# A third buffer for the doubled queries in the second attention block of a diffusion-backbone layer on one Trainium2 core

## The chip, the cores and the metric

One core of one Trainium2 chip runs the whole kernel in one launch. The metric is device time in microseconds (us), the median of several runs. Engines are named as in the profile: PE (TensorE), DVE (VectorE), ACT (ScalarE), POOL (GpSimd), and SP, which here only issues DMAs.

## What is computed

One layer over 256 context tokens and 2048 latent tokens (a grid of 32 rows by 64 columns), model width 1024, float32. An input projection feeds three mixers: 2-D neighbourhood attention, a gated recurrence in both directions and a short convolution. They are merged by sigmoid gates and projected out. The change concerns the neighbourhood attention of the latent tokens alone:

```python
# 8 heads of 64; windows of 8 rows x 16 columns; queries in blocks of 16 columns
s_loc = einsum('brnqhd,brnikhd->brnhqik', q_blk, k_band)       # 8 x 32 keys around the block
s_ctx = einsum('brnqhd,bchd->brnhqc', q_blk, ctx_k)            # 256 cached context keys
s = concatenate([s_loc * scale + bias, s_ctx * scale], -1)     # learned bias per head, mask
p = softmax(s, -1)
o = p_loc @ v_band + p_ctx @ ctx_v
```

## The kernel before

**Precision.** Every dense product splits its operands into a high and a low part and sums three passes. For attention scores, queries are stored in DRAM as `d_q[512, 2, T]`, each row holding the high and the low part. The function `twice` (L654) reads one head's rows twice, so that all 128 partitions hold them: these are the doubled queries `qs`, a tile of 128 x 2 x 512 floats, 512 KB. The keys `kd` hold high parts in partitions 0 to 63 and low parts in 64 to 127.

**Two blocks.** [...] The first block's attention has query group 0 alone (pool `atA`); the second block's (pool `atB`) has groups 1, 2 and 3. A group is 8 grid rows, 512 queries. A job is one group of one head, in the order of `jobs` (head 0 groups 1, 2, 3, then head 1 and so on: 24 jobs), written here as (group, head). A job has four units, one for each block of 16 columns (b = 0 to 3).

**A unit** (`attend1` and on): PE computes the scores `sc` against the context keys (L583) and `sl` against the local keys (L587), both from `qs`; DVE moves them out of PSUM with a row maximum (L588, and L590, which adds the bias `bt`); ACT takes the exponential (L596); DVE scales by the reciprocal sum (L598). Two units later PE transposes the probabilities `p` (L611), ACT copies them out (L614), and after that PE multiplies them with the values (L624) into `o`. `fin` (L757) multiplies a job's `o` with its gate `sg` on DVE (L762) and stores `zt`.

**Loads.** All loads of this stage are issued from POOL's queue. After unit b = 0 of a job, the loads of the next job are written: `load_group` (L725) loads `qs`, for a new head's group 1 and group 3 the bias `bt`, and the gate `sg`; at a change of head `load_head` (L711) comes first with `kd` and the cached keys `ck`, and `load_values` (L720) follows after b = 3. Tiles of `atB` have two buffers by default; `sg` has three. A load waits for the last reader of the buffer that it overwrites, and whatever stands behind it in POOL's queue waits too. POOL also computes the low parts of the dense weights (`wlo`, L56).

**Order of the work.** The attention units are put between the dense column tiles 40 + m, m = 4 to 17 (`ps`, L153, 24 matmuls for each of two token chunks) by `Side`, 101 steps over 27 chunks. The framework's scheduler then fixes one order for each engine's queue, from its own costs and from which buffers it expects to be free; at run time each engine works its queue in that order.

Of the kernel before, what the change touches and what calls it, by code (L numbers as in the profile page):

```python
# [9 lines left out]
F32R = mybir.dt.float32r  # L10
# [5 lines left out]
P = 128  # L16
# [28 lines left out]
def build(nc, tc, H):  # L45
# [5 lines left out]
    def r2f(ap):  # L51
        return ap.bitcast(F32)
# [598 lines left out]
    def rows(h):  # L651
        return slice(h * HD, h * HD + HD)

    def twice(h, t0, n):  # L654
        return d_q[rows(h), :, t0 : t0 + n].unsqueeze(0).broadcast_to([2, HD, 2, n])
# [46 lines left out]
    def latent_steps(at, gs):  # L702

        cv = at.tile([P, 2, 512], F32, tag="cv", name=f"cv{gs[0]}", bufs=1)
        row0 = GR[gs[0]][1]
        nrows = GR[gs[-1]][1] + GR[gs[-1]][2] - row0
        nrow_max = max(GR[g][2] for g in gs)
        nq = (nrows + 3) // 4
        heads, groups, bias = {}, {}, {}

        def load_head(h):  # L711

            kd = at.tile([P, nrows * 64], F32R, tag="kd", name=f"kd{row0}_{h}")
            t0 = 256 + row0 * 64
            G.dma_start(r2f(kd), d_k[h, :, :, t0 : t0 + nrows * 64].rearrange("a p n -> (a p) n"))
            ck = at.tile([P, 256], F32R, tag="ck", name=f"ck{row0}_{h}")
            G.dma_start(r2f(ck), d_ck[h].rearrange("a p n -> (a p) n"))
            heads[h] = [kd, ck, None]

        def load_values(h):  # L720
            vb = at.tile([P, nq, 4, HD], F32, tag="vb", name=f"vb{row0}_{h}")
            G.dma_start(vb, d_vb[h][:, row0 // 4 : row0 // 4 + nq])
            heads[h][2] = vb

        def load_group(g, h):  # L725
            _, _, nrow, bi = GR[g]
            qs = at.tile([P, 2, 512], F32R, tag="qs", name=f"qs{g}_{h}")
            G.dma_start(r2f(qs), twice(h, 256 + 512 * g, 512))
            if (bi, h) not in bias:
                bt = at.tile([P, 3, nrow_max * 32], F32, tag="bt", name=f"bt{bi}_{h}")  # L730
                G.dma_start(bt[:, :, : nrow * 32], H[f"bias{bi}"][h])
                bias[bi, h] = bt
            sg = at.tile([HD, 512], F32, tag="sg", name=f"sg{g}_{h}", bufs=3)
            G.dma_start(sg, d_gna[rows(h), 256 + 512 * g : 768 + 512 * g])
            groups[g, h] = qs, bias[bi, h], sg

        jobs = [(g, h) for h in range(HEADS) for g in gs]

        def first_loads():
            load_head(0)  # L740
            load_group(*jobs[0])
            G.dma_start(cv, H["cv"].rearrange("(a p) c -> p a c", p=P))
            load_values(0)

        return first_loads, latent_units(at, jobs, heads, groups, cv, row0, load_head, load_group, load_values)

    def latent_units(at, jobs, heads, groups, cv, row0, load_head, load_group, load_values):
# [163 lines left out]
    with tc.tile_pool(name="zp", bufs=2, reuse_waits="tile") as zp:  # L911
        for c in (0, 1, 2, 3, 4):
# [5 lines left out]
            for br in (2, 1, 0):  # L918
# [6 lines left out]
                for m in range(8):  # L925
                    t = zp.tile([P, 512], F32, tag="acc" if br == 2 else "tg", name=f"tg{c}_{br}_{m}",
                                bufs=9 if br == 2 else 6)
# [148 lines left out]
```

## Time and profile before

| | us |
|---|---|
| median of 3 runs (lowest to highest) | 2610.14 (2605.08 to 2614.53) |
| the profiled execution's own time | 2611.47 |
| its span, first to last instruction | 2609.7 |
| mean granted TensorE clock, share of full | 0.985 |
| second block's attention, where it runs beside the dense tiles | about 1576 to 2025 of the span |
| loads of `qs` in the profile | 32 (8 in the first block, 24 in the second) |

Times in rows are us from the start of the span. The span is some 2 us shorter than the execution's own time. [...] Where a row says that an engine was idle until something, that is the event that came last by the profile.

### The profile page before, as it was taken

To read this page: it belongs to the slowest core of one execution; us is meant where nothing else is said; L and a number is where in the kernel's file an instruction comes from. 1 tells how busy PE (TensorE), PEld (TensorE's weight loads), DVE (VectorE), ACT (ScalarE), POOL (GpSimd) and SP (SyncE) were. 2 spreads that over 40 slices of the span, in tenths; PEclk is the share of its full clock that TensorE was granted. 3 is DMA by queue.
4 is the path that set the end of the run, shared out by engine and by line. 5 is a ranking of instruction groups with operands and counts; after the bars stand their busy time and mean duration, and the time that the engine had idled before them with its cause. 6 is when DMAs were issued, how large, how long until landed. Compare 5 with 4: busy or idle time off the path is not lost.

```text
span 2609.7 us, 35312 instructions
## 1 busy us (share of the span) xinstructions
PE 2542.3 (97%) x13192; PEld 2077.4 (80%) x13192; DVE 1104.2 (42%) x2329; ACT 978.3 (37%) x1849; POOL 876.7 (34%) x757
## 2 busy tenths in 40 slices
PE   8999999999999999999999997999999999999998
PEld 4887788888878888888888886777777888888887
DVE  5101245555123331325777863455444134333433
ACT  4312443444223334436665653444444311111221
POOL 2311223323532321522544443233231413334642
PEclk9999999999999999999999998999899999999999
DMA  7335642332733434435642335455442466545442
GB/s 275 112 87 159 170 122 81 68 70 69 188 106 119 148 121 145 133 101 135 190 156 91 115 121 179 136 146 151 131 137 77 155 224 200 177 157 186 159 141 88
DMA packets 248812, 360.84 MB, mean 138 GB/s; under 512 B 88761, under 2 KB 124729, under 8 KB 247617
## 3 DMA queue, kind: packets, MB, share of 16 engines
q1 hardware_dynamic: 147360, 227.20, 28.7%
q0 software_dynamic: 47920, 64.26, 8.8%
q10 hardware_dynamic: 53360, 67.13, 7.8%
q8 instruction: 104, 1.70, 0.3%
q14 instruction: 68, 0.55, 0.1%
HBM read 248.10 MB, written 110.11 MB: 137 GB/s over the span
## 4 chain that ended last, share of the span: by engine, by line
PE 75%; DMA 6%; issue 4%; POOL 2%; DVE 1%; ACT 0%; SPq 0%; ACTq 0%; POOLq 0%; DVEq 0%
PE ps L153 45%; PE pb L932 12%; PE po L981 8%; DMA qs<-d_q 3%; PE t L611 3%; PE o L624 2%; PE pg L454 2%; PE pv L321 1%; PE sl L587 1%; PE sc L583 1%; DMA bt<-bias 1%; DMA d_z<-sp 1%; POOL wlo L56 0%; DMA kp<-d_k 0%; DMA d_q<-evl 0%
## 5 line engine op out<-in xcount | busy, mean ns | idle before, releaser
L153 PE MATMUL ps<-xh,whi 128*128 128x512 f32 (+1 forms) x2400 | 899.6, 375 | 0.0
L153 PE MATMUL ps<-xl,whi 128*128 128x512 f32 (+1 forms) x2400 | 888.8, 370 | 2.4 <-DVE xl L56 1.6
L153 PE MATMUL ps<-xh,wlo 128*128 128x512 f32 (+1 forms) x2400 | 888.2, 370 | 0.0
L153 PEld LDWEIGHTS ps<-xh,whi 128*128 128x128 f32 x2400 | 455.2, 190 | 93.7 <-issue 6.2
L56 POOL TENSOR_TENSOR wlo<-wraw,whi 128x512 fp32r<-128x512 f32 x240 | 334.0, 1409 | 570.0 <-ACT whi L55 505.3
L153 PEld LDWEIGHTS ps<-xh,wlo 128*128 128x128 f32 x2400 | 455.1, 190 | 78.1
L153 PEld LDWEIGHTS ps<-xl,whi 128*128 128x128 f32 x2400 | 455.2, 190 | 77.8 <-POOL xl L56 2.0
L55 ACT CAST whi<-wraw 128x512 fp32r<-128x512 f32 x240 | 144.8, 616 | 300.1 <-PE ps L153 160.9
L932 PE MATMUL pb<-zh,wbh 128*128 128x512 f32 (+1 forms) x480 | 179.0, 373 | 4.3 <-ACT zh L55 4.3
L167 ACT ACTIVATE evm<-ps 128x512 f32<-128x512 f32 (+1 forms) x120 | 66.3, 552 | 301.1 <-PE ps L153 300.2
L932 PE MATMUL pb<-zl,wbh 128*128 128x512 f32 (+1 forms) x480 | 179.1, 373 | 0.0
L932 PE MATMUL pb<-zh,wbl 128*128 128x512 f32 (+1 forms) x480 | 179.0, 373 | 0.0
L588 DVE TENSOR_SCALAR_CACHE_REDUCE p<-sc 128x256 f32<-128x256 f32 x127 | 53.9, 424 | 254.1 <-PE sc L583 253.1
L939 POOL TENSOR_TENSOR tg<-tg,tg 128x512 f32<-128x512 f32 (+1 forms) x80 | 96.9, 1221 | 188.5 <-DVE tg L935 184.3
L935 DVE SCALAR_TENSOR_TENSOR tg<-tg,pb 128x512 f32<-128x512 f32 (+1 forms) x120 | 74.7, 631 | 151.8 <-PE pb L932 139.8
L611 PE MATMUL t<-ident,p 128*128 128x128 f32 (+1 forms) x698 | 129.4, 286 | 7.0 <-DVE ast L595 3.4
L611 PEld LDWEIGHTS t<-ident,p 128*128 128x128 f32 (+1 forms) x698 | 91.6, 142 | 53.9 <-issue 19.6
L614 ACT COPY pT<-t 128x512 f32<-128x512 f32 (+3 forms) x256 | 96.2, 406 | 75.0 <-PE t L611 74.7
L596 ACT ACTIVATE p<-p,ast 128x736 f32<-128x736 f32 (+2 forms) x127 | 109.4, 862 | 39.5 <-DVE ast L595 38.1
L444 DVE SCALAR_TENSOR_TENSOR uf<-ut,pk,uf 128x512 f32<-128x512 f32 (+1 forms) x120 | 103.0, 858 | 30.5 <-ACT uf L441 28.6
L475 POOL TENSOR_TENSOR sq<-sq,ea 128x512 f32<-128x512 f32 (+1 forms) x40 | 61.9, 1548 | 154.2 <-ACT sq L468 92.6
L55 ACT CAST zh<-zr 128x512 fp32r<-128x512 f32 (+1 forms) x60 | 30.5, 575 | 211.8 <-PE pb L932 92.6
(233 smaller groups left out, 3689.7 us busy)
## 6 DMA issues: line engine op xcount, KB each, us to landing
wraw<-w_in SPq DMA_DIRECT2D x240, 256.0 KB, 3.4
d_sig<-evm ACTq DMA_DIRECT2D x96, 256.0 KB, 3.5
tg<-d_sig SPq DMA_DIRECT2D x96, 256.0 KB, 3.8
xt<-x SPq DMA_DIRECT2D x36, 512.0 KB, 3.7
qs<-d_q POOLq DMA_DIRECT2D x32, 512.0 KB, 17.1
zr<-d_z SPq DMA_DIRECT2D x12, 1024.0 KB, 5.4
d_mrg<-tg ACTq DMA_DIRECT2D x32, 256.0 KB, 4.4
mr<-d_mrg SPq DMA_DIRECT2D x8, 1024.0 KB, 5.8
```

The lines of the kernel that those rows point to most:

```text
L55: S.copy(hi, src)
L56: lo_eng.tensor_tensor(lo, src, r2f(hi), ALU.subtract)
L153: TE.matmul(ps[:, :n], (lo if a else hi)[:, k, :], (xl if b else xh)[ci][:, k, :], start=(i == 0), stop=(i == len(ps_) - 1))
L167: S.activation(o[:, :n], ps, AF.Tanh, scale=0.5)
L444: V.scalar_tensor_tensor(uf[:, :n], ut[:, tap : tap + n], cw(tap), uf[:, :n], ALU.mult, ALU.add)
L596: S.activation(p[:, :nk], p[:, :nk], AF.Exp, bias=st[:, 2:3], accum_out=st[:, 3:4])
L611: TE.transpose(tb[:, off : off + w], p[q0:q1, c0 : c0 + P], ident[q0:q1, q0:q1])
L614: S.copy(pT[:, base : base + off], tb[:, :off])
L932: TE.matmul(ps[:, :n], (wbl if a_ else wbh)[br * 4 + k][:, m * P : (m + 1) * P], (zl if b_ else zh)[:, k, :n], start=(i == 0), stop=(i == ...
L935: V.scalar_tensor_tensor(t[:, :n], t[:, :n], 1.0, ps[:, :n], ALU.add, ALU.mult)
L939: G.tensor_tensor(acc[m][:, :n], acc[m][:, :n], t[:, :n], ALU.add)
L981: TE.matmul(ps, (ml if a_ else mh)[:, k, j * P : (j + 1) * P], (wol if b_ else woh)[k][:, hs], start=(i == 0), stop=(i == len(ps_) - 1))
```

## The change

`qs` gets three buffers instead of two where the stage has more than one group, that is, in the second block; the first block keeps two.

```diff
         def load_group(g, h):
             _, _, nrow, bi = GR[g]
-            qs = at.tile([P, 2, 512], F32R, tag="qs", name=f"qs{g}_{h}")
+            qs = at.tile([P, 2, 512], F32R, tag="qs", name=f"qs{g}_{h}",
+                         bufs=3 if len(gs) > 1 else 2)
             G.dma_start(r2f(qs), twice(h, 256 + 512 * g, 512))
```

One line is added, so lines behind L728 have numbers higher by one. The queues of PE, DVE, ACT and SP hold the same instructions in the same order as before. On POOL's queue the loads of `qs` move. The number of instructions is the same on every engine.

POOL's queue around the change from head 0 to head 1, before (`qs2_1` is the load of `qs` for group 2 of head 1):

```order
L56 TENSOR_TENSOR wlo47_14386<-wraw47_0_14387,whi47_14385 128x512
L728 DMA qs3_0_13682<-d_q_57 128x2x512
L56 TENSOR_TENSOR wlo47_14386<-wraw47_1_14391,whi47_14385 128x512
L734 DMA sg1_1_13863<-d_gna_62 64x512
L728 DMA qs1_1_13859<-d_q_57 128x2x512
L731 DMA bt1_1_13861<-bias1 128x1440
L734 DMA sg2_1_14021<-d_gna_62 64x512
L717 DMA ck4_2_14352<-d_ck_59 128x256
L728 DMA qs2_1_14019<-d_q_57 128x2x512
L731 DMA bt2_1_14189<-bias2 128x3x384
L715 DMA kd4_2_14350<-d_k_58 128x1792
```

And in the changed kernel:

```order
L729 DMA qs1_1_13859<-d_q_57 128x2x512
L56 TENSOR_TENSOR wlo47_14386<-wraw47_0_14387,whi47_14385 128x512
L56 TENSOR_TENSOR wlo47_14386<-wraw47_1_14391,whi47_14385 128x512
L735 DMA sg1_1_13863<-d_gna_62 64x512
L729 DMA qs2_1_14019<-d_q_57 128x2x512
L732 DMA bt1_1_13861<-bias1 128x1440
L735 DMA sg2_1_14021<-d_gna_62 64x512
L717 DMA ck4_2_14352<-d_ck_59 128x256
L729 DMA qs3_1_14187<-d_q_57 128x2x512
L732 DMA bt2_1_14189<-bias2 128x3x384
L715 DMA kd4_2_14350<-d_k_58 128x1792
```

To within a row or two, each place that held a load of `qs` still holds one, but that of the next job: where `qs1_1` stood in front of `bt1_1`, `qs2_1` stands now; where `qs2_1` stood behind `ck4_2`, `qs3_1` stands now. So each load of `qs` is moved ahead of the rows that stood between two of them. The same pattern holds for the later heads.

The first loads of the stage, POOL's queue before:

```order
L722 DMA vb4_0_13362<-d_vb_61 128x1792
L728 DMA qs2_0_13548<-d_q_57 128x2x512
L734 DMA sg2_0_13550<-d_gna_62 64x512
L731 DMA bt2_0_13684<-bias2 128x3x384
L734 DMA sg3_0_13686<-d_gna_62 64x512
L715 DMA kd4_1_13855<-d_k_58 128x1792
```

And in the changed kernel:

```order
L722 DMA vb4_0_13362<-d_vb_61 128x1792
L729 DMA qs2_0_13548<-d_q_57 128x2x512
L735 DMA sg2_0_13550<-d_gna_62 64x512
L729 DMA qs3_0_13682<-d_q_57 128x2x512
L732 DMA bt2_0_13684<-bias2 128x3x384
L735 DMA sg3_0_13686<-d_gna_62 64x512
```

Here the third load of `qs` goes out with the first batch, ahead of the second bias table.

## Rows read from the trace of the kernel before

**Rows 1.** The page: busy time of the engines; the chain that ended last.
```profile
PE 2542.3 (97%) x13192; PEld 2077.4 (80%) x13192; DVE 1104.2 (42%) x2329; ACT 978.3 (37%) x1849; POOL 876.7 (34%) x757
PE ps L153 45%; PE pb L932 12%; PE po L981 8%; DMA qs<-d_q 3%; PE t L611 3%; PE o L624 2%; PE pg L454 2%; PE pv L321 1%; PE sl L587 1%; PE sc L583 1%; DMA bt<-bias 1%; DMA d_z<-sp 1%; POOL wlo L56 0%; DMA kp<-d_k 0%; DMA d_q<-evl 0%
```
**Rows 2.** Waits of PE, 1620 to 2025: us in total, times, longest.
```profile
PE sc L583 <- DMA qs<-d_q: 11.5, 5, 3.4
PE t L611 <- DVE p L598: 3.4, 8, 1.6
PE sc L583 <- DVE ast L595: 2.4, 1, 2.4
```
**Rows 3.** PE's timeline: start, us, what, [idle before <-releaser].
```profile
1668.27 0.76 PE L583 MATMUL sc<-ck,qs 128*128 128x256 f32 x2 [3.37 <-DMA qs<-d_q]
...
1719.91 0.47 PE L583 MATMUL sc<-ck,qs 128*128 128x256 f32 x2 [2.38 <-DVE ast L595]
...
1875.52 0.77 PE L583 MATMUL sc<-ck,qs 128*128 128x256 f32 x2 [3.38 <-DMA qs<-d_q]
...
1931.91 0.48 PE L583 MATMUL sc<-ck,qs 128*128 128x256 f32 x2 [2.79 <-DMA qs<-d_q]
...
1981.84 0.47 PE L583 MATMUL sc<-ck,qs 128*128 128x256 f32 x2 [1.53 <-DMA qs<-d_q]
```
**Rows 4.** POOL's timeline around the change from head 0 to head 1.
```profile
1632.96 2.12 POOL L728 DMA_DIRECT2D qs<-d_q  x1 [4.92 <-PE sl L587]
1635.07 0.57 POOL L731 DMA_DIRECT2D bt<-bias  x1
...
1648.53 2.10 POOL L728 DMA_DIRECT2D qs<-d_q  x1 [0.60 <-PE t L611]
```
**Rows 5.** Tile `qs`, 1620 to 2025, from issue to landing.
```profile
DMA to landing us min/median/max: 14.8/16.3/20.4
```
**Rows 6.** Windows: stretch, its us, busy us and count by engine, PEclk, DMA share, GB/s.
```profile
1620.00:2025.00 405.00, 383.29 (x2577) 300.44 (x2575) 195.32 (x687) 180.41 (x424) 109.48 (x100) 0.95 0.44 129
1668.30:1688.30 20.00, 19.76 (x121) 15.15 (x121) 9.06 (x34) 8.49 (x20) 4.69 (x3) 0.87 0.35 96
1719.90:1739.90 20.00, 19.99 (x121) 15.74 (x121) 8.77 (x30) 7.59 (x18) 2.20 (x3) 0.83 0.30 91
1875.50:1895.50 20.00, 19.98 (x97) 15.10 (x98) 7.17 (x26) 6.78 (x16) 0.68 (x2) 0.59 0.23 70
1931.90:1951.90 20.00, 19.75 (x130) 15.20 (x132) 9.54 (x36) 9.20 (x22) 5.39 (x5) 0.91 0.35 103
1981.80:2001.80 20.00, 19.96 (x146) 16.05 (x146) 9.93 (x37) 8.95 (x20) 0.47 (x1) 0.91 0.20 62
...
1755.00:1765.00 10.00, 10.00 (x56) 8.19 (x57) 3.08 (x11) 2.52 (x8) 1.11 (x2) 0.83 0.81 204
```
**Rows 7.** The chain, 1560 to 2030: 24 value matmuls at either clock.
```profile
1671.46 2.17 PE o L624 x24
...
1688.60 1.26 PE o L624 x24
```
**Rows 8.** DVE's L598, 1620 to 2025: duration in ns, min/median/max.
```profile
L598 DVE TENSOR_SCALAR p<-p,ast x93: 533/600/2092, 1621.3 to 2014.6; 128x736 f32<-128x736 f32 x61, 128x640 f32<-128x640 f32 x32
```
**Rows 9.** Timelines of POOL, DVE and PE: an issue, a scaling, a transpose.
```profile
1717.30 2.12 POOL L728 DMA_DIRECT2D qs<-d_q  x1 [0.78 <-PE t L611]
1717.81 1.95 DVE L598 TENSOR_SCALAR p<-p,ast 128x736 f32<-128x736 f32 x1
...
1980.58 1.50 DVE L598 TENSOR_SCALAR p<-p,ast 128x736 f32<-128x736 f32 x1
...
1787.60 1.21 PE L611 MATMUL t<-ident,p 128*128 128x128 f32 x6 [1.55 <-DVE p L598]
```
**Rows 10.** Tile `bt`, 1620 to 2025: who waited for it; from issue to landing.
```profile
  DVE p L590: 3.8, 4
DMA to landing us min/median/max: 14.7/17.3/20.1
```

## The prediction

> **What bounds the kernel now.** I read the page first: PE is busy for 97% of the span, and the chain that ended last is mostly its matmuls, but 3% of it is the load of `qs` [rows 1]. That share is a pointer, not a price: a chain can run through a load beside which PE works. So I went to the one stage where these loads matter, 1620 to 2025, and asked what PE itself waits for. There PE is busy 383.3 of 405 us and its mean granted clock is 0.95 [rows 6]: 21.7 us idle, and some 5% of the time lost in clock. Of the idle time 11.5 us are waits of the score matmul `sc` for the load of `qs`, and 2.4 us more are a wait of `sc` put down to DVE [rows 2].
>
> Then the timeline, wait by wait. Five `sc` start late by 1.5 to 3.4 us [rows 3]; counting scores in PE's order, each is unit b = 0 of a group 2: jobs (2,1), (2,2), (2,5), (2,6), (2,7). Why group 2 is seen on POOL [rows 4]: the load at 1648.53 is that of (2,1). Its buffer was last read by (3,0), whose last scores PE had only just issued, and PE wants the new `qs` one job later. Its landing is what the first row of [rows 3] waits for, 19.7 us after the issue; loads of `qs` take 14.8 us at the least and 20.4 at the most [rows 5]. A job lasts about as long: the loads at 1632.96 and 1648.53 are 15.6 us apart. With two buffers a load has one job's time to land, and that is no margin.
>
> **What the change does, part by part.**
>
> *The loads leave a job sooner.* POOL's place behind `ck` now issues `qs` of (3,h), and (2,h) goes out in the place where (1,h) went, at 1632.96 in this trace: 15.6 us sooner for (2,1). PE idles from 1664.90 (1668.27 less 3.37), 16.4 us after the old issue; after the new one that is 32.0 us, against 20.4 us for the slowest landing. The margin is over 11 us, and it holds at the other heads, as the queue repeats. So I take the five waits as gone: 3.37 + 2.38 + 3.38 + 2.79 + 1.53 = **13.5 us** [rows 3].
>
> *The clock after them.* Behind each of the five waits the granted clock falls. The 20 us behind them show 0.87, 0.83, 0.59, 0.91 and 0.91 [rows 6]. [...] If PE no longer waits, I expect the clock to stay up. The bounds are nothing of it and all of it; I take all, less what follows.
>
> *What comes to light.* Under the wait at 1719.91 lies another: DVE's L598 took 1.95 us instead of the usual 0.60 [rows 8, 9]. It began 0.5 us after POOL started to issue a load of `qs`, an instruction of 2.12 us, and ended with it. The row shows only that they overlap and that DVE loses; four L598 of the stage, the first of them this one and the last at 1980.58 with 1.50 us, are stretched beside such an issue. [...] Where a collision is not covered, PE shows what it costs: 1.55 us idle at 1787.60 [rows 9], and after another such case a clock of 0.83 over 10 us [rows 6], 3.4 us at the lower level, 1.4 us lost: 3.0 us in all. Two of the five waits (1719.91 and 1981.84) cover a stretched L598; I count both as uncovered: **6.0 us given back**. Bounds: none, if the shifted times miss each other, and two more.
>
> *Small waits for probabilities.* PE's transposes wait for L598 eight times, 3.4 us, of it 1.55 the case above [rows 2], so 0.26 us each. Without the five pauses there may be one more each: **1.3 us given back**.
>
> *Costs of nothing.* Instructions, bytes and DMAs are the same. `wlo`, `sg` and `ck` that `qs` is moved past are issued in the same places to within one 2.1 us issue; the covers are a weight tile made ahead into one of three buffers and a gate not needed until its job's end. If a weight tile were late, PE would lose at most those 2.1 us once. Where the queue now waits (for the last scores of the job before, in front of `bt`), it waited before for the same event [rows 4]. In the first batch the third `qs` (512 KB) takes the place of a bias table (576 KB) that is not wanted before the third job: nothing, or the 2.1 us of one issue either way. The stages behind are shifted, not changed.
>
> **The sum.** 13.5 + 15.0 - 6.0 - 1.3 = 21.2 us. The profiled execution took 2611.5 us, which gives 2590.3; it stands 1.3 us above the median of the runs, so against the median I forecast **2589 us** (0.8% less).
>
> **The rivals.**
>
> *More than forecast (0.13).* If neither collision comes to light, the two that already cost PE time go as well, and the one small wait for `qs` at a head change (11.5 us [rows 2] less the four shown [rows 3] leaves 0.4) vanishes: 28.5 + 6.0 + 0.4 = 34.9 us, 2575 us. Against it: nothing in the change removes an issue.
>
> *The bias tables take over (0.12).* `bt` of group 1 has two buffers and the same trigger, one job ahead: it is issued at 1635.07, right behind a `qs` [rows 4], and lands after 14.7 to 20.1 us; DVE already waits for it four times, 3.8 us [rows 10], at most 1.6. PE's pace between trigger and need is the same as before, since the pauses that go lie elsewhere, so I expect no more of it. If each of seven head changes waited the longest seen, 7 x 1.6 = 11.2 us would go back: 2600 us.
>
> *The load is hidden anyway, or leaves no sooner (0.08).* Then nothing changes: 2610 us. [...] For this rival speaks only that the 2.4 us wait is put down to DVE.
>
> *Slower, by collisions (0.05).* Uncovered issues of `qs` on L598 cost 3.0 us each. From ten more of them on (28.5 / 3.0 = 9.5) the gain is gone; if 21 issues all collided where two now cost PE time, 19 x 3.0 = 57 us against 28.5, 2639 us. For it: an issue's start follows PE's scores, and DVE's chain follows the same scores, so they can fall into step. Against it: the triggers are the events of before, with which only four met.
>
> **How the numbers follow.** The forecast has 0.62. What a measurement here can tell from no change is about 0.3%, 7.8 us. Faster by more: the forecast, the larger gain and most of the bias case, 0.62 + 0.13 + 0.10 = 0.85. Within it: the hidden load and the ends of the others, 0.11. Slower: 0.04. The range runs from 2573, the larger gain and the 2.1 us of an issue, to a gain of 11.1 us (the waits named to the load, without clock) less 6.0 for the collisions, 2605: that holds the forecast, the larger gain and the bias case but for their edges.
>
> **What would show it.** In the changed profile `sc` no longer waits for `qs`, and the five starts at group 2 have no gap; loads of `qs` land 10 us and more ahead of use. The stage is shorter by 15 to 30 us and its clock at 0.98 or more, where it was 0.95. Waits on `bt` stay below 6 us, and some L598 still last near 2 us beside an issue. I am wrong if the gaps at `sc` remain, if `bt` or `p` takes their whole place, or if the clock stays at 0.95 without them.

## The result, and the profile after

The changed kernel takes **2583.26 us** (median of 4 runs, 2583.09 to 2587.91), the kernel before on the same chip 2610.87 (median of 4, 2605.08 to 2614.53): a ratio of 0.990, 95% interval 0.9882 to 0.9918. The profiled execution took 2583.13 us, 28.3 us less than that of before.

The page, busy time and chain, answers to [rows 1]:

```profile
PE 2525.7 (98%) x13192; PEld 2064.8 (80%) x13192; DVE 1103.8 (43%) x2329; ACT 977.8 (38%) x1849; POOL 879.0 (34%) x757
PE ps L153 48%; PE pb L933 12%; PE po L982 8%; PE t L611 3%; PE o L624 2%; PE pg L454 2%; PE pv L321 2%; PE sl L587 1%; PE sc L583 1%; DMA bt<-bias 1%; DMA qs<-d_q 1%; DMA d_z<-sp 0%; POOL wlo L56 0%; DMA kp<-d_k 0%; DMA d_q<-evl 0%
```

The same instructions keep PE busy for 16.6 us less, and the load of `qs` has 1% of the chain instead of 3%. PE's waits in the stage, now 1620 to 1998 (us in total, times, longest; these two are all that the view lists), answer to [rows 2]:

```profile
PE t L611 <- DVE ast L595: 6.5, 4, 2.3
PE t L611 <- DVE p L598: 4.4, 9, 1.6
```

There is no wait of `sc` left. PE's timeline shows the start of job (2,1), which answers to the first of [rows 3] and has no idle time before it, and the places where PE does idle:

```profile
1653.33 0.86 PE L611 MATMUL t<-ident,p 128*128 128x128 f32 x5 [2.35 <-DVE ast L595]
...
1664.46 0.51 PE L583 MATMUL sc<-ck,qs 128*128 128x256 f32 x2
...
1701.17 0.86 PE L611 MATMUL t<-ident,p 128*128 128x128 f32 x5 [1.10 <-DVE p L598]
...
1743.93 0.86 PE L611 MATMUL t<-ident,p 128*128 128x128 f32 x5 [1.69 <-DVE ast L595]
...
1775.74 1.21 PE L611 MATMUL t<-ident,p 128*128 128x128 f32 x6 [1.55 <-DVE p L598]
...
1895.61 0.86 PE L611 MATMUL t<-ident,p 128*128 128x128 f32 x5 [2.35 <-DVE ast L595]
```

POOL's timeline, as [rows 4]: the load of (2,1) goes out at 1632.56, in the place of (1,1).

```profile
1632.56 2.11 POOL L729 DMA_DIRECT2D qs<-d_q  x1 [5.49 <-PE t L611]
1634.67 0.57 POOL L732 DMA_DIRECT2D bt<-bias  x1
...
1646.95 2.10 POOL L729 DMA_DIRECT2D qs<-d_q  x1
```

It is no faster on the way; tile `qs`, 1620 to 1998, answers to [rows 5]:

```profile
DMA to landing us min/median/max: 15.2/16.5/19.9
```

The load issued at 1632.56 lands at 1648.72, by its event in the trace, and is read at 1664.46. From job (2,0) on the loads land 8 to 24 us ahead of use. The stage's very first load, ahead of these windows, is as late as before: its `sc` waits 8.8 us at 1598.59. The windows, with the columns of [rows 6]: the stage, and 20 us behind four of the places above.

```profile
1620.00:1998.00 378.00, 366.68 (x2578) 287.99 (x2575) 192.49 (x687) 178.95 (x421) 107.08 (x99) 1.00 0.46 137
1653.30:1673.30 20.00, 19.73 (x128) 15.26 (x129) 9.74 (x35) 8.96 (x21) 3.56 (x3) 1.00 0.64 191
1743.90:1763.90 20.00, 19.97 (x147) 15.97 (x148) 11.98 (x44) 10.60 (x25) 4.78 (x6) 1.00 0.70 195
1775.70:1795.70 20.00, 19.96 (x133) 15.89 (x134) 9.95 (x37) 8.77 (x21) 4.89 (x7) 1.00 0.36 105
1895.60:1915.60 20.00, 19.75 (x128) 15.28 (x129) 9.72 (x35) 8.96 (x21) 3.56 (x3) 1.00 0.64 196
```

The stage is 27 us shorter for the same 2,578 matmuls (2,577 recorded before). Busy time and idle time of PE split that gain:

| 1620 to 2025 before, to 1998 after | before | after | gain | forecast |
|---|---|---|---|---|
| PE idle | 21.7 | 11.3 | 10.4 | 13.5 - 2 x 1.55 - 1.3 = 9.1 |
| PE busy (the same work, clock 0.95 and 1.00) | 383.3 | 366.7 | 16.6 | 15.0 - 2 x 1.45 = 12.1 |
| sum | 405 | 378 | 27.0 | 21.2 |

DVE's side: the waits on `bt` answer to [rows 10]. The second row names another engine in front of the same operation, at 1699.33; that table landed at 1699.17, by its event, so this wait of 1.8 us belongs to the tables as well, 7.1 us in all against 3.8 before.

```profile
DVE p L590 <- DMA bt<-bias: 5.3, 3, 2.5
DVE p L590 <- PE sc L583: 1.8, 1, 1.8
...
1650.58 0.72 DVE L590 CUSTOM_DVE_ANT_0 p<-sl,bt,ast 128x480 f32<-128x480 f32 x1 [2.51 <-DMA bt<-bias]
1891.87 0.72 DVE L590 CUSTOM_DVE_ANT_0 p<-sl,bt,ast 128x480 f32<-128x480 f32 x1 [1.53 <-DMA bt<-bias]
```

For the first of these, job (1,1), a row of PE before the change matters as well; `qs` of that job landed at 1648.74 then, by its event:

```profile
1648.83 0.48 PE L583 MATMUL sc<-ck,qs 128*128 128x256 f32 x2 [0.77 <-ACT whi L55]
```

The stretched scalings, as [rows 9], DVE and POOL: two beside an issue of `qs`, one beside POOL's `wlo` (two such rows are put together in one).

```profile
1741.79 2.09 DVE L598 TENSOR_SCALAR p<-p,ast 128x640 f32<-128x640 f32 x1
1741.47 2.11 POOL L729 DMA_DIRECT2D qs<-d_q  x1
...
1773.75 1.94 DVE L598 TENSOR_SCALAR p<-p,ast 128x736 f32<-128x736 f32 x1
1773.24 2.11 POOL L729 DMA_DIRECT2D qs<-d_q  x1 [2.02 <-PE sl L587]
...
1893.91 1.65 DVE L598 TENSOR_SCALAR p<-p,ast 128x640 f32<-128x640 f32 x1
1892.70 2.50 POOL L56 TENSOR_TENSOR wlo<-wraw,whi 128x512 fp32r<-128x512 f32 x2
```

The first two are the pauses of 1.69 and 1.55 us. Before, PE paused at the same two places, for 1.69 us at 1754.28 and 1.55 us at 1787.60 [rows 9]:

```profile
1754.28 0.86 PE L611 MATMUL t<-ident,p 128*128 128x128 f32 x5 [1.69 <-DVE ast L595]
```

The clock fell behind both then, in 20 us each:

```profile
1754.30:1774.30 20.00, 20.00 (x142) 15.91 (x142) 10.84 (x39) 9.52 (x23) 4.71 (x6) 0.91 0.65 181
1787.60:1807.60 20.00, 20.00 (x126) 15.77 (x127) 9.28 (x36) 8.76 (x21) 3.21 (x4) 0.91 0.35 105
```

### The profile page after: what moved, and what is told of

The parts are those of the page before. It is cut to its first block, busy times and chain, and to the rows that moved or that the text cites. A ratio compares the mean times of both kernels' runs of the same rounds, so it can differ in the third digit from the quotient of the medians.

```text
span 2581.3 us, 35325 instructions
## 1 busy us (share of the span) xinstructions
PE 2525.7 (98%) x13192; PEld 2064.8 (80%) x13192; DVE 1103.8 (43%) x2329; ACT 977.8 (38%) x1849; POOL 879.0 (34%) x757
## 4 chain that ended last, share of the span: by engine, by line
PE 80%; DMA 4%; issue 2%; DVE 1%; POOL 1%; ACT 0%; SPq 0%; ACTq 0%; DVEq 0%; POOLq 0%
PE ps L153 48%; PE pb L933 12%; PE po L982 8%; PE t L611 3%; PE o L624 2%; PE pg L454 2%; PE pv L321 2%; PE sl L587 1%; PE sc L583 1%; DMA bt<-bias 1%; DMA qs<-d_q 1%; DMA d_z<-sp 0%; POOL wlo L56 0%; DMA kp<-d_k 0%; DMA d_q<-evl 0%
## 5 line engine op out<-in xcount | busy, mean ns | idle before, releaser
L611 PE MATMUL t<-ident,p 128*128 128x128 f32 (+1 forms) x698 | 125.3, 279 | 11.3 <-DVE ast L595 6.5
L611 PEld LDWEIGHTS t<-ident,p 128*128 128x128 f32 (+1 forms) x698 | 89.1, 139 | 56.4 <-issue 16.6
```

What stands on the lines that cost most here:

```text
L611: TE.transpose(tb[:, off : off + w], p[q0:q1, c0 : c0 + P], ident[q0:q1, q0:q1])
```

## The experiments

The theory: a load of `qs` takes about a whole job or more to land (14.8 to 20.4 us [rows 5] against 15.6), so with two buffers PE waits for it, and each wait is paid twice, as idle time and as clock. One more buffer ends both. The rivals: the gain comes from the shifted queue or the clock without the waits; the bias tables limit as much; or the count of buffers is beside the point and the slow load is the cause. The kernels ran on several chips, so each is told by its ratio to the kernel before on its own chip; the number in brackets is the 95% interval.

**The changed kernel once more**, on another chip.

> The changed kernel once more, as the measure for the others of this call on one chip, since four buffers came out at 2597 us on another chip. If three buffers are really better than four, it is 25 to 30 us under the kernel before here too. If the difference lay in the chip, it comes near the 17 us of four buffers.

Measured: 2587.77 us against 2612.97, 0.9919 (0.9902 to 0.9937). The result repeats. PE's pauses stand at the same places with nearly the same lengths (2.35, 1.39, 1.69, 1.56, 2.34), but for one more of 2.42 us at 1945.56, behind which the clock falls (0.91 over 20 us).

**Four buffers.**

```diff
-                         bufs=3 if len(gs) > 1 else 2)
+                         bufs=4 if len(gs) > 1 else 2)
```

> Four buffers of the doubled queries instead of three. If two buffers merely gave a load too little time to land, three are enough: the loads of the changed kernel already land 8 to 24 us ahead of their score matmul, so the time stays at 2583 us, 4 either way. If depth as such pays (earlier loads also free the queue behind them), another 5 us or more go: 2578 or less.

Measured: 2597.05 us against 2613.63, 0.9931 (0.9905 to 0.9957). That is above the expected 2583, give or take 4; by the ratios it can't be told from three buffers. From job (1,1) on the loads land 20 to 39 us ahead, which is of no use. Waits of PE, 1620 to 2000, show 14.3 us at the transposes instead of 10.9:

```profile
PE t L611 <- DVE ast L595: 7.0, 5, 2.7
PE t L611 <- DVE p L598: 5.7, 9, 1.8
PE t L611 <- DVE ast L597: 1.6, 1, 1.6
```

DVE waits 10.1 us for the bias tables, at most 5.2, and eight L598 last longer than 1.4 us, where the changed kernel has three. Whether the earlier loads push the tables back was not shown by a run of its own. The profiled run (2589.95 us) is the shortest of the four, so what the others lost is not in the trace.

**A third buffer for the bias tables**, with and without that of `qs`.

```diff
-                bt = at.tile([P, 3, nrow_max * 32], F32, tag="bt", name=f"bt{bi}_{h}")
+                bt = at.tile([P, 3, nrow_max * 32], F32, tag="bt", name=f"bt{bi}_{h}",
+                             bufs=3 if len(gs) > 1 else 2)
```

> Three buffers for the bias tables, two for the queries. If the queries' load was the cause, its five long pauses (13.5 us) and the lower clock behind them (15 us) stay, and only two pauses of 0.9 and 0.6 us can go: 2608 to 2611 us. If what helped was any relief of POOL's queue or of the waits at a change of head, a good part of the 28 us comes here too: 2595 us or less.

> Three buffers for the bias tables too, beside three for the queries. If the bias table is what is late next, the three pauses of TensorE behind it (2.35, 1.10 and 2.35 us, 5.8 us in all) go: about 2577 us. If it only hides the next late thing, 2583 us as now.

Measured: tables alone 2615.84 us against 2613.63, 1.0014 (0.9996 to 1.0032); both 2585.14, 0.9889 (0.9868 to 0.9911). With the tables alone the waits that the theory names stay, 16.2 us of PE in 1620 to 2000:

```profile
PE sc L583 <- DMA qs<-d_q: 16.2, 6, 5.0
```

So the tables do not limit by themselves. On top of `qs` they take the pauses at 1653 and 1895 from 2.35 to 0.90 us each, but the expected 2577 us is not reached; the difference to the change is within the intervals.

**The waits filled with useless work.** 14 matmuls of 128x512 into the bank that the scores overwrite, in front of the five starts of [rows 3]: in the kernel before, and in the changed one.

```diff
+        if nm in ("1_2_0", "2_2_0", "5_2_0", "6_2_0", "7_2_0"):
+            for i in range(14):
+                TE.matmul(sc_, xh[3][:, i % 8, 0:P], xh[3][:, i % 8, :], start=(i == 0), stop=(i == 13))
```

> Two buffers as before, but TensorE gets 14 matmuls without use (128 x 512 each, about 3.2 us) in front of the first scores of jobs (2,1), (2,2), (2,5), (2,6) and (2,7), where it waited 13.5 us in all. They add 15.9 us of work, 2.4 more than the pauses that they fill. If the clock falls because TensorE pauses, it stays up: 2611 - 15 + 2.4 = 2598 us. If the clock fell for another reason, nothing is won: 2613 us.

> The changed kernel with the same 5 x 14 matmuls without use as in the run that filled the pauses. Here nothing waits at these places, so the whole 15.9 us lie on TensorE's path: 16 us over the changed kernel of this call, some 12 us under the kernel before. With that the filled run of before can be read: if the queries' waits cost idle time and clock and nothing else, filled pauses and no pauses but the same filling take the same time (within 4 us). If filling in the kernel before came out slower than this, waits remain there that the filling did not reach.

Measured: before with the filler 2610.13 us against 2613.63, 0.9981 (0.9964 to 0.9997); changed with the filler 2604.58 against 2612.97, 0.9975 (0.9958 to 0.9992). Some 16 us of extra work (an estimate: the `ps` matmuls of this size start 0.23 us apart in the trace of before, at 1707.67 and on) cost the changed kernel 16.8 us, and the kernel before nothing (3.5 us less between the medians, a ratio just below 1 by its interval). With the filler the two kernels are equal: it makes no difference how many buffers there are once PE works through the waits. The expected 2598 us of the first was missed all the same, by 12 us. The window 1620 to 2000 of the filled kernel before:

```profile
1620.00:2000.00 380.00, 370.20 (x2554) 291.83 (x2553) 193.91 (x680) 176.34 (x412) 111.55 (x101) 1.00 0.47 136
```

Its clock is 1.00 where [rows 6] have 0.95. In this run useless work in place of a pause of about the same length gave the clock back, so the lower clock of [rows 6] was a consequence of the pauses, not of the stage's work. This run is the shortest of its ten (2600.83 us), and what the stage of the others did is not shown. Over the whole execution the ten have a clock of 0.988 to 0.992, the kernel before on that chip 0.982 to 0.989. So the clock is higher with the filler, but the time fell by less than was expected of that.

**Loads of `qs` issued by SP**, with two and with three buffers. POOL's issue of 2.1 us goes, and so should the stretched L598.

```diff
-            G.dma_start(r2f(qs), twice(h, 256 + 512 * g, 512))
+            (SY if len(gs) > 1 else G).dma_start(r2f(qs), twice(h, 256 + 512 * g, 512))
```

> Two buffers, but the doubled queries are loaded from SP's queue instead of POOL's. If the cause is that a load has one job of about 15.6 us and takes 15 to 20, a load that lands in 10 us or less needs no third buffer: the waits of the scores go as with three buffers, 28 us; and since POOL no longer issues these loads, the two scalings that collide with an issue (3.2 us) and most of the waits for the bias tables (5.8 us), whose loads go out sooner and alone, go too: 30 to 37 us under the kernel before. If SP's queue, which also brings the weights and takes the outputs, is held up by a load that waits for its buffer, weights come late and half of it or more is lost: 15 us or less.

> Three buffers and loads from SP's queue. If two buffers on SP already have the loads landed in time, the third adds nothing: within 3 us of the run with two on SP. If loads on SP still land late, it is faster than that by what waits are left there.

Measured: two buffers 2632.04 us against 2612.97, 1.0092 (1.0071 to 1.0112), slower; three 2606.12, 0.9978 (0.9968 to 0.9988). The expectation for two buffers was missed. With two buffers, SP's and PE's timelines:

```profile
1711.69 0.51 SPq L728 DMA_DIRECT2D qs<-d_q  x1
...
1734.73 0.55 PE L583 MATMUL sc<-ck,qs 128*128 128x256 f32 x1 [7.16 <-DMA qs<-d_q]
```

From issue to use it is 23.0 us, and 17 to 24 at the other waits in 1620 to 2000: another queue did not make the load faster. PE waits eight times for `qs` there, 27.5 us in all, and 19.0 us at the stage's first `sc` (9.0 before). The longest wait of PE for an L598 is 0.3 us there, where it was 1.6. With three buffers the waits for `qs` in the stage are gone as well. But the first `sc` waits 19.8 us (8.8 in the changed kernel), and PE pauses 5.6 us for a copy of ACT and 3.8 us for an L598 at two places, with a clock of 0.97 in the stage: 18.4 us more than the changed kernel on the same chip. So the time of the load is not POOL's doing.

**Loads cut in two along the partitions.** A window of the kernel before near the end of its load of 1632.96, which lands at 1648.74, with the rests of others under way as well (the bias table issued behind it lands at 1650.43, a gate at 1650.96); columns of [rows 6], the last two DMA share and GB/s:

```profile
1645.50:1648.30 2.80, 2.56 (x15) 1.99 (x13) 1.06 (x4) 1.62 (x3) 0.56 (x1) 1.00 0.13 53
```

A share of 0.13 of 16 engines is about two of them at work (0.13 x 16 = 2.1), at 53 GB/s. 512 KB at that rate would take 9.9 us without any waiting, an estimate. The access is `[2, 64, 2, 512]`: its outermost dimension is the doubling. That this 2 holds the load to two engines was the author's assumption, which the trace of before does not show; a load of 64 rows into 64 partitions puts it to the test. With two buffers:

```diff
-            G.dma_start(r2f(qs), twice(h, 256 + 512 * g, 512))
+            for a in (0, 1):
+                G.dma_start(r2f(qs[a * HD : a * HD + HD]), d_q[rows(h), :, 256 + 512 * g : 768 + 512 * g])
```

> Two buffers as before, but each load of doubled queries is cut into two loads of 64 partitions with 256 KB each, so that no access pattern begins with a dimension of 2. If a load takes 15 us and more because its outermost dimension of 2 spreads it over few DMA engines, the halves land in 8 us or less, and the scores' waits go without a third buffer; the bias tables behind them land sooner too, and POOL's issues get shorter: 30 to 40 us under the kernel before. If the 512 KB simply take that long with all else that is under way, the halves land as late as the whole did, and the time is that of the kernel before, 3 us either way.

Measured: **2568.43 us** against 2613.30, 0.9834 (0.9817 to 0.9851). Tile `qs`, then `bt`, 1620 to 2000:

```profile
DMA to landing us min/median/max: 3.5/4.9/8.8
DMA to landing us min/median/max: 4.3/6.5/7.0
```

These are the halves; a pair is there 5.8 us (median) after its first issue, where the whole load took 16.3, and the bias tables, issued right behind it, land in 6.5 us instead of 17.3. The wait of 9.0 us at the stage's first `sc` and the pauses by POOL's issues (an issue now takes 0.6 us) are gone too, so more than the five waits is gained.

> The cut loads and three buffers. If the cut loads land in 8 us or less, a job's time is margin enough and the third buffer adds nothing: within 3 us of two buffers with cut loads. If they land late, it gains over them what the third buffer gained over the kernel before, 25 us.

Cut loads and three buffers: 2565.50 us, 0.9823 (0.9806 to 0.9841). The third buffer, worth 21 to 28 us with the slow load, is worth 3 between the medians with the fast one, which is within the intervals, as the theory has it.

> Two buffers with the cut loads, and the doubled queries of the context tokens (first block) cut too. The first block's stage has some 6 us of idle TensorE, part of it behind those loads: 0 to 5 us less than with cut loads of the latent queries alone. No theory of the change hangs on it; it tells whether the same cut pays elsewhere.

Two buffers, and the doubled queries of the context tokens (line 665, the same kind of load, in the first block) cut as well: **2560.12 us**, 0.9799 (0.9781 to 0.9816), 8.3 us better than the cut of `qs` alone, more than expected. This beats both kernels, the changed one by some 1%. The gain lies in the first block, where these queries are used; the cut of `qs` alone, then both cuts:

```profile
640.00:780.00 140.00, 132.90 (x732) 113.07 (x731) 32.84 (x109) 41.72 (x98) 58.61 (x60) 0.98 0.53 144
640.00:780.00 140.00, 139.49 (x782) 119.31 (x781) 38.69 (x120) 43.36 (x102) 52.55 (x68) 1.00 0.54 151
```

PE idles 7.1 us there with one cut and 0.5 with both, and the clock goes from 0.98 to 1.00: idle time and clock once more.

**Cut in two along the other dimension.** Each part still doubles its rows.

```diff
-            G.dma_start(r2f(qs), twice(h, 256 + 512 * g, 512))
+            for c in (0, 1):
+                G.dma_start(r2f(qs[:, c]), d_q[rows(h), c, 256 + 512 * g : 768 + 512 * g].unsqueeze(0).broadcast_to([2, HD, 512]))
```

> Two buffers. Each load of qs is cut in two as in the run with cut loads, 256 KB each, but along the other dimension: each part still fills all 128 partitions by reading 64 rows twice, so its outermost dimension stays 2. While such a load alone is in flight before, the DMA share is 0.13, two of 16 engines, at 53 GB/s. Theory (the outer dimension of 2 sends the load to two engines): the parts are no quicker together than the whole, the second lands 13 us and more after the first issue, the share of a part alone stays near 0.13 or is 0.25 if the two fall to different engines; time within 15 us of before, 2595 to 2620 us. Rival (any cut into 256 KB pieces helps, because there are two transfers): both land within 5 to 6 us, as with the cut into halves of partitions, and the time is 2568 us.

Measured: 2578.45 us against 2616.55, 0.9853 (0.9831 to 0.9874). Neither expectation held in full. Tile `qs`, and a window while a pair is in flight:

```profile
DMA to landing us min/median/max: 8.8/10.1/12.3
...
1634.50:1636.00 1.50, 1.50 (x23) 1.35 (x20) 1.31 (x6) 1.50 (x5) 0.00 (x0) 1.00 0.25 86
```

A part of 256 KB takes twice as long as one cut along the partitions (10.1 against 4.9 us), and the pair has a share of 0.25, about four engines of 16. Both cuts make parts of 256 KB; the slow one keeps the 2 outermost, as the theory has it. But the two parts go side by side, so the pair is there 10.9 us (median) after the first issue, 13.3 at most, within the 15.6 us of a job, and that is enough for nearly all of the gain. The time is near the rival's, some 5 us above it by the ratios (0.9853 against 0.9834), since what counts here is whether the load is there within a job, not how fast it is.

## Why the prediction was right

It said 2589 us; 2583.3 were measured, inside the range. The mechanism was right: the five waits and the clock behind them. The two deductions were not, and their errors cancel in part. By its steps:

- **Five waits, 13.5 us: right.** All are gone, and those loads land 15.7 us and more ahead of use. The run with the bias tables alone and the cut loads show that the late load was the cause.
- **The clock, 15.0 us: right, and all of it.** PE's busy time fell by 16.6 us at a clock of 1.00. No run shows the 15.0 us by themselves: they are an estimate from two levels of the clock, 0.50 and 1.00. Of the 400 windows of 1 us from 1620 to 2020 in the trace of before, 349 show 1.00, 37 show 0.50 and 14 lie between. Two stretches, with the columns of [rows 6]:

```profile
1880.00:1890.00 10.00, 10.00 (x61) 7.46 (x61) 4.27 (x16) 3.64 (x9) 0.00 (x0) 0.50 0.14 49
...
1900.00:1910.00 10.00, 10.00 (x87) 8.36 (x87) 6.03 (x23) 5.10 (x14) 1.02 (x2) 1.00 0.47 129
```

With these levels the five stretches of 20 us in [rows 6] have 35.6 us at 0.50, and 0.91 of each 2.17 us is lost there [rows 7]. In place of the estimate the runs showed the 16.6 us. The filled kernel before shows that the pauses brought the clock down (1.00 instead of 0.95 in the stage). That the clock did not fall once is in part luck, see below.

- **What comes to light, 6.0 us given back: mis-sized, it is 0.** This was the step "I count both as uncovered". No run shows the 3.0 us for each by themselves either: 1.55 are idle time [rows 9], and 1.4 are the clock by the same estimate, from 0.83 over 10 us [rows 6]. The two collisions that cost PE time before cost it again (1.69 and 1.55 us), but the two that had lain under waits did not appear: there the shifted issues missed L598. The lower bound that the prediction gave, "none, if the shifted times miss each other", is what happened. Of the 4.5 us between 16.6 and 12.1, 2.9 are the clock that was set down for these two. The remaining 1.6 fit the two collisions that remain: before, the clock fell behind both (0.91 over 20 us each, 0.83 in the 10 us of [rows 6]), now it is 1.00. One reading was off: the L598 at 1717.81 ends at 1719.76, 0.34 us behind POOL's issue and not with it, and so do the two now (0.30 and 0.34).
- **Small waits, 1.3 us given back: the place was wrong.** The pauses at transposes grew from 6.8 to 10.9 us in total, 4.1 us, and mostly for bias tables: 2.35 us at 1653.33, 1.10 at 1701.17, and part of the 2.35 at 1895.61. So the step "PE's pace between trigger and need is the same as before, since the pauses that go lie elsewhere" failed. The table of (1,1) lands at 1650.4 in both traces; DVE wanted it at 1649.84 before (waited 0.75 us) and wants it at 1648.07 now. Part of this is a pause that lay between trigger and need, and went. Before, PE stood idle at the first `sc` of (1,1) itself, for 0.77 us until 1648.83; the profile puts this down to ACT, but the job's `qs` had only landed at 1648.74. Now that `sc` starts at 1647.02. The sign "waits on `bt` stay below 6 us" holds by the view's 5.3, but not by the 7.1 us with the wait at 1699.33. This rival has a seed of truth, but stayed far from its 11.2 us of PE time.
- **Costs of nothing: right** where a place shows it: no row has PE waiting for a weight tile, `sg` or `ck`.

The two errors have opposite signs: 6.0 us too little gained, against 2.8 too much. Slower by collisions did not come about: there are as many issues, and two met L598 at PE's cost.

That the load is hidden anyway is refuted: none of these loads lands in less than 14.8 us [rows 5], about a job's 15.6 us, and with the waits for them gone the kernel takes 27.6 us less.

**What stays open.** Why the clock fell behind pauses of 1.5 to 3.4 us before and behind none of the pauses of 1.10 to 2.35 us now is not settled. In the changed kernel with the filler PE pauses for 2.35 us at the same transpose, at 1654.56, and the clock falls behind it:

```profile
1654.60:1674.60 20.00, 20.00 (x123) 15.89 (x124) 8.01 (x29) 7.39 (x17) 3.56 (x3) 0.91 0.63 188
```

So a pause of this size may or may not cost clock.

## What to carry to other kernels

Where a wait at one place comes back at each turn of a loop, compare the time from issue to landing with the time that the buffers allow, here 16 us against a job of 15.6; a buffer more was a cure at that margin (21 to 28 us), and was worth 3 us, within the intervals, once the load was in time. Then ask why the load takes so long: a DMA share of 0.13 while little else is under way, or a small outermost dimension in its access, pointed here to a cut of the load that is worth more than the buffer (45 us, and 53 with the context queries cut too, instead of 21 to 28). Price a pause of PE with the clock behind it: here the clock was more than half of the gain.

## What was not expected of the hardware

- The doubled load of 512 KB showed a DMA share of 0.13, about two of 16 engines, at 53 GB/s, and took 15 to 20 us from POOL's queue and, where PE waited for it, 17 to 24 us to its use from SP's. Cut into two of 64 partitions, each half landed in 3.5 to 8.8 us.
- What was issued right behind the slow load on the same queue was late as well: the bias tables fell from a median of 17.3 us to 6.5 when it was cut, and to 8.5 when it went to SP's queue.
- 14 useless matmuls in each of five pauses cost the kernel before nothing (2610.13 us against 2613.63), and in the profiled run they gave the clock back (0.95 to 1.00 in the stage).
- An L598 of DVE was stretched beside POOL's `wlo` as others were beside an issue (2.09 and 1.94 us), to 1.65 us at 1893.91; one of the same 128x640 at 1700.56 took 0.55.
